# Gate and up of 512 features as one 2x2 block product: seven products in three of eight k-tile pairs, eight PSUM banks, three parts

## The chip, the cores and the metric

The kernel runs on one core of one Trainium2 chip. The metric is the device time of one execution in microseconds (us). Engines are named as in the profile: PE is TensorE, DVE is VectorE, ACT is ScalarE, POOL is GpSimd, SP is the engine that issues most DMAs.

## The reference

Two transformer-like blocks run one after the other on 256 tokens of 2048 features, in float32. The stage that is changed is the feed-forward part of the first block:

```python
h2 = _rmsnorm(x, ffn_norm_w[l])
g, u = jnp.split(jnp.einsum('bsd,df->bsf', h2, w_gate_up[l]), 2, axis=-1)
x = x + jnp.einsum('bsf,fd->bsd', jax.nn.silu(g) * u, w_down[l])
```

`w_gate_up` is 2048 x 11264 (gate in the first 5632 columns, up in the rest), `w_down` is 5632 x 2048. Before this stage stand a gated recurrence, a short convolution and the output projection `w_out`; after it come a second block with attention and a long convolution, and a last norm.

## The kernel before

Every large product is computed with operands split into two float32r parts, high and low: `x = xh + xl`, `w = wh + wl`, and `x w` is taken as `xh wh + xh wl + xl wh`. The split of a weight tile is made on the chip: SP loads 512 KB (two k-tiles of 128 rows by 512 columns) into a `raw` buffer, ACT rounds it into `wh` (L63, by way of `act`), and DVE writes `wl = raw - wh` (L54, by way of `tt`). `split` (L105) does this. It runs at a priority raised by 4000, so that the planner, which orders each engine's list at build time, puts it ahead of the ordinary work. There are four `wh`/`wl` buffer pairs (`wsp`), and four `raw` buffers, eight in the feed-forward stage (`wraw`, `wraw2`, taken in turn).

There are two forms of the product. `proj` (L132) keeps tokens on the output's partitions: the token tile is the stationary operand, the weights move, and each token half takes three 512-column matmuls per k-tile (L149 to L151). `proj_t` (L160) keeps features on the output's partitions: a 128 x 128 block of the weights is stationary, and the high and low parts of all 256 tokens move past it in one matmul of 512 columns (L177), then the low weights meet the high tokens in one of 256 columns (L178; L174 and L175 for the last k-tile). `proj_t` then adds the two halves of its four banks by one ACT copy and one DVE addition each (L182, L183).

The feed-forward stage (L592 to L622) walks 11 groups f of 512 features, in two parts of six and five. For each f it calls `proj_t` for gate, multiplies by the token scale `rs1b` (the reciprocal root of the norm, spread along the free axis by L217), applies Silu, calls `proj_t` for up, multiplies, and splits h into a unit `u` (high and low parts, four k-tiles by 256 tokens). After each part, `proj` multiplies the part's units with `w_down` for four chunks of 512 output columns, and `residual` (L574) adds the result to `X` on DVE. The norm weight is folded into the units `x1u`, which `unit_from` (L87) builds from transposes of `X` (L82) chunk by chunk in the output projection.

PSUM has eight banks: five in `pmm` (matmul results of `proj` and `proj_t`) and three in `phd` (transposes, small products; taken by `bank`). `proj_t` takes four banks at a time, `proj` two.

## Time and profile before

| what | us |
|---|---|
| median of three runs | 1621.42 (1620.3 to 1622.43) |
| the profiled execution | 1621.36 |
| its span (first to last instruction) | 1619.7 |
| PE busy | 1605.1 (99%) |
| DVE busy | 1099.3 (68%) |
| ACT busy | 845.6 (52%) |

The profile lists, for each group of instructions of one line and shape, the count, the busy time, the mean duration and the idle time of the engine just ahead of them with what ended it. The timeline lists instructions by start, neighbours of one group merged into one line with a count. Durations of pipelined instructions overlap, so the spacing of starts tells what one of a stream costs. The windows give the busy time of each engine in a stretch; the column PEclk is the granted clock as a share of 2.4 GHz.

### The profile page before, as it was taken

The page shows a single profiled execution, that of the slowest core. Times are in us where ns is not written, and L with a number is a line of the kernel's source. Part 1 is how long each engine was busy: PE and PEld are TensorE (multiplying, and loading weights), DVE is VectorE, ACT ScalarE, POOL GpSimd, SP SyncE. Part 2 cuts the span into 40 slices and gives each one's busy share as a digit, 9 for nine tenths or more (in the row PEclk, how much of TensorE's full clock was granted, in tenths as well). Part 3 has the DMA queues.
Part 4 walks back from the last instruction along what each step waited for, and adds up shares of the span by engine and source line. Part 5 has one row for each costly group of instructions (what it writes and reads, how often), then busy time and mean ns, then how long its engine had stood idle before and what let it go on. Part 6 is the DMA issues. An engine that isn't in the chain of part 4 may idle for free. (4 is left out here: it accounts for less than half of the span.)

```text
span 1619.7 us, 23619 instructions
## 1 busy us (share of the span) xinstructions
PE 1605.1 (99%) x9152; PEld 1448.8 (89%) x9152; DVE 1099.3 (68%) x1495; ACT 845.6 (52%) x1125; POOL 21.2 (1%) x57
## 2 busy tenths in 40 slices
PE   8999999999999999999999999999999999999998
PEld 7999999999988999999888999998889889998987
DVE  8769768765766666666554566665658999766854
ACT  5657557544544554545444454545446445655743
POOL 2000000000000000000000000000000000000000
PEclk9999999999999999999999999999999999999999
DMA  8765565556696666665666566666547567656564
GB/s 291 219 196 156 152 186 170 152 176 206 208 308 212 193 199 204 198 200 193 216 201 203 183 207 208 207 200 202 197 144 247 157 194 217 188 156 195 165 214 142
DMA packets 166897, 318.45 MB, mean 197 GB/s; under 512 B 12248, under 2 KB 13168, under 8 KB 166784
## 3 DMA queue, kind: packets, MB, share of 16 engines
q1 hardware_dynamic: 164304, 312.19, 61.1%
q10 hardware_dynamic: 2032, 4.60, 0.8%
q8 instruction: 72, 1.18, 0.3%
q14 instruction: 41, 0.34, 0.1%
q0 software_dynamic: 448, 0.14, 0.1%
HBM read 313.74 MB, written 3.15 MB: 196 GB/s over the span
## 5 line engine op out<-in xcount | busy, mean ns | idle before, releaser
L54 DVE TENSOR_TENSOR wl<-raw,wh 128x1024 fp32r<-128x1024 f32 (+1 forms) x580 | 700.8, 1220 | 434.3 <-ACT wh L63 430.4
L63 ACT ACTIVATE wh<-raw 128x1024 fp32r<-128x1024 f32 (+1 forms) x580 | 603.9, 1054 | 603.4 <-PE p L177 268.4
L177 PE MATMUL p<-u,wh 128*128 128x512 f32 x2712 | 891.0, 383 | 0.8 <-DVE sg L54 0.6
L178 PE MATMUL p<-u,wl 128*128 128x256 f32 x2712 | 712.7, 274 | 1.0 <-DVE wl L54 0.9
L177 PEld LDWEIGHTS p<-u,wh 128*128 128x128 f32 x2712 | 507.0, 189 | 61.0 <-DVE sg L54 1.1
L178 PEld LDWEIGHTS p<-u,wl 128*128 128x128 f32 x2712 | 519.3, 191 | 13.8 <-DVE wl L54 1.7
L150 PE MATMUL p<-wl,u 128*128 128x512 f32 x736 | 281.2, 383 | 0.0
L151 PE MATMUL p<-wh,u 128*128 128x512 f32 x736 | 277.7, 380 | 1.9 <-DVE u L51 1.9
L149 PE MATMUL p<-wh,u 128*128 128x512 f32 x736 | 277.7, 382 | 1.1 <-ACT u L63 0.6
L149 PEld LDWEIGHTS p<-wh,u 128*128 128x128 f32 x736 | 139.1, 189 | 21.1 <-ACT u L63 1.6
L151 PEld LDWEIGHTS p<-wh,u 128*128 128x128 f32 x736 | 138.8, 189 | 21.3 <-DVE u L51 2.7
L150 PEld LDWEIGHTS p<-wl,u 128*128 128x128 f32 x736 | 139.3, 189 | 19.4 <-DVE wl L54 0.7
L175 PE MATMUL p<-u,wh 128*128 128x512 f32 x184 | 70.7, 384 | 0.0
L63 ACT ACTIVATE low<-p 128x256 f32<-128x256 f32 x184 | 64.1, 375 | 8.7 <-DVE sg L54 1.5
L51 DVE SCALAR_TENSOR_TENSOR acc<-up,cw,acc 128x256 f32<-128x256 f32 x120 | 51.1, 470 | 0.7 <-ACT acc L63 0.7
L174 PE MATMUL p<-u,wl 128*128 128x256 f32 x184 | 50.7, 275 | 0.0
L174 PEld LDWEIGHTS p<-u,wl 128*128 128x128 f32 x184 | 34.8, 189 | 4.8
L149 PE MATMUL p<-wh,x 128*128 128x512 f32 x96 | 36.4, 379 | 0.0
L150 PE MATMUL p<-wl,x 128*128 128x512 f32 x96 | 36.4, 379 | 0.0
L151 PE MATMUL p<-wh,x 128*128 128x512 f32 x96 | 36.4, 379 | 0.0
L54 DVE TENSOR_TENSOR g<-g,rs1b 128x1024 f32<-128x1024 f32 x22 | 27.0, 1225 | 12.7 <-ACT g L63 12.3
L175 PEld LDWEIGHTS p<-u,wh 128*128 128x128 f32 x184 | 35.3, 192 | 0.1
(272 smaller groups left out, 937.5 us busy)
## 6 DMA issues: line engine op xcount, KB each, us to landing
raw<-in_w_in_dram SPq DMA_DIRECT2D x232, 512.0 KB, 4.1
raw<-in_w_gate_up_dram SPq DMA_DIRECT2D x176, 512.0 KB, 4.6
raw<-in_w_down_dram SPq DMA_DIRECT2D x88, 512.0 KB, 4.6
raw<-in_w_out_dram SPq DMA_DIRECT2D x64, 512.0 KB, 4.8
raw<-in_w_mem_kv_dram SPq DMA_DIRECT2D x14, 512.0 KB, 5.8
xp<-in_x_dram SPq DMA_DIRECT2D x4, 512.0 KB, 7.0
X<-in_x_dram SPq DMA_DIRECT2D x4, 512.0 KB, 5.6
mp<-in_mem_dram SPq DMA_DIRECT2D x3, 512.0 KB, 7.5
```

The source lines that it names most:

```text
L51: nc.vector.scalar_tensor_tensor(out=out, in0=in0, scalar=scalar, in1=in1, op0=op0, op1=op1)
L54: nc.vector.tensor_tensor(out=out, in0=a, in1=b, op=op)
L63: nc.scalar.activation(out=out, in_=in_, func=func, **kw)
L149: nc.tensor.matmul(pt[t], lhsT=u[:, k, 0, sl], rhs=mh, start=st, stop=False)
L150: nc.tensor.matmul(pt[t], lhsT=u[:, k, 0, sl], rhs=ml, start=False, stop=False)
L151: nc.tensor.matmul(pt[t], lhsT=u[:, k, 1, sl], rhs=mh, start=False, stop=sp)
L174: nc.tensor.matmul(pt[f][:, :T], lhsT=wl[:, a, fs], rhs=high, start=False, stop=False)
L175: nc.tensor.matmul(pt[f], lhsT=wh[:, a, fs], rhs=both, start=False, stop=True)
L177: nc.tensor.matmul(pt[f], lhsT=wh[:, a, fs], rhs=both, start=st, stop=False)
L178: nc.tensor.matmul(pt[f][:, :T], lhsT=wl[:, a, fs], rhs=high, start=False, stop=False)
```

## The change

Gate and up of one f are computed together, with tokens on the output's partitions (the form of `proj`). For a pair of k-tiles the product is seen as a 2x2 block product: the blocks of the left side are the two token halves by the two k-tiles, those of the right side the two k-tiles by gate and up. Pairs 0, 1, 3, 5 and 6 are multiplied plainly, eight block products each. Pairs 2, 4 and 7 are multiplied by Strassen's scheme in Winograd's form, seven block products each. The products of all pairs add up in eight banks, P1 to P7 and X4: a plain pair adds straight into P2 and P4 (gate) and P3 and X4 (up).

The sums of token blocks (`F`) are made once, in the output projection, from the transposes that make `x1u`. The differences of weight blocks (`Ta`, `Tb`) are made by DVE for each f after the load, in `raw` buffers, and then split like weights. At the end of an f, nine operations combine the eight banks into g and u. h then has tokens on its partitions, so it is transposed on PE ahead of the last pair of the next f, in the bank of X4, whose partial sum has been copied out before. The token scale is now a scalar per partition, and `rs1b` goes. The split weights get two more buffer pairs (`wsx`), the `fp` pool has one buffer where it had two, and the 11 groups run in three parts of four, four and three.

```diff
-    def split(w, r0, nk, c0, n, pool=wsp):
+    def load(w, r0, nk, c0, n):
+        raw = raw_tile(nk, n)
+        nc.sync.dma_start(
+            out=raw, in_=w[r0:r0 + nk * 128, c0:c0 + n].rearrange("(k p) n -> p k n", p=128)
+        )
+        return raw
+    def parts_of(raw, pool=None):
+        if pool is None:
+            pool = more_w[0] if more_w else wsp
+            if more_w:
+                more_w.append(more_w.pop(0))
+        wh = pool.tile(list(raw.shape), F32R, tag="wh", name="wh")
+        wl = pool.tile(list(raw.shape), F32R, tag="wl", name="wl")
+        act(wh, raw)
+        tt(wl, raw, wh.bitcast(F32), ALU.subtract)
+        return wh, wl
+    def split(w, r0, nk, c0, n, pool=None):
         with tc.high_priority(4000):
...
+            return parts_of(load(w, r0, nk, c0, n), pool)
...
+    def seven_forms(c):
+        def keep(j, ps):
+            p = 2 * c + j
+            if p not in (2, 4, 7):
+                return
+            x_ = fp.tile([128, CW], F32, tag="s1", name="xs").rearrange("p (a t) -> p a t", a=2)
+            for a in range(2):
+                act(x_[:, a], ps[:, a], scale=col("ffn", 2 * p + a))
+            (a11, a21), (a12, a22) = ((x_[:, a, :128], x_[:, a, 128:]) for a in range(2))
+            s_ = fp.tile([128, CW], F32, tag="u2", name="ss").rearrange("p (i t) -> p i t", i=4)
+            tt(s_[:, 0], a21, a22, ALU.add)
+            tt(s_[:, 1], s_[:, 0], a11, ALU.subtract)
+            tt(s_[:, 2], a11, a21, ALU.subtract)
+            tt(s_[:, 3], a12, s_[:, 1], ALU.subtract)
+            F = fp.tile([128, 4, 2, 128], F32R, tag=f"F{p}", name=f"F{p}")
+            act(F[:, :, 0], s_)
+            tt(F[:, :, 1], s_, F[:, :, 0].bitcast(F32), ALU.subtract)
+            sums7[p] = F
...
-        x1u.append(unit_from(xk(c), lambda k, c=c: col("ffn", 4 * c + k)))
+        x1u.append(unit_from(xk(c), lambda k, c=c: col("ffn", 4 * c + k), keep=seven_forms(c)))
...
-    rs1b = along_free(rs1, fp, "rs1b")
     more_raw.extend([wraw, ff.enter_context(tc.tile_pool(name="wraw2", bufs=4))])
+    wsx = ff.enter_context(tc.tile_pool(name="wsx", bufs=2))
+    more_w.extend([wsp, wsp, wsx, wsp, wsp, wsx])
+    def tri(pt, left, right, st, sp):
+        (xh, xl), (wh, wl) = left, right
+        mh, ml = in_turn(wh), in_turn(wl)
+        nc.tensor.matmul(pt, lhsT=xh, rhs=mh, start=st, stop=False)
+        nc.tensor.matmul(pt, lhsT=xh, rhs=ml, start=False, stop=False)
+        nc.tensor.matmul(pt, lhsT=xl, rhs=mh, start=False, stop=sp)
+    def hidden_pre(f, before_last):
+        P1, P2, P6, P7, P5 = [mm_bank() for i in range(5)]
+        P3, P4, X4 = [bank([128, CW]) for i in range(3)]
...
+        for p in order:
...
+            if p not in sums7:
+                for (b0, b1), c0 in (((P2, P4), f * CW), ((P3, X4), DFF + f * CW)):
+                    wh, wl = split(w_gate_up, r0, 2, c0, CW)
+                    for a in range(2):
+                        for t, b in enumerate((b0, b1)):
+                            prod(b, x_(a, t), (wh[:, a], wl[:, a]), b is X4 and p == last_plain and a == 1)
+                continue
+            if end:
+                x4 = fp.tile([128, CW], F32, tag="x4", name="x4")
+                with tc.high_priority(4000):
+                    act(x4, X4)
+                before_last(X4)
+            F = sums7[p]
+            with tc.high_priority(4000):
+                g_ = load(w_gate_up, r0, 2, f * CW, CW)
+                u_ = load(w_gate_up, r0, 2, DFF + f * CW, CW)
+                B1 = parts_of(g_)
+                Ta, Tb = raw_tile(2, CW), raw_tile(2, CW)
+                tt(Ta[:, 0], u_[:, 0], g_[:, 0], ALU.subtract)
+                tt(Ta[:, 1], u_[:, 1], u_[:, 0], ALU.subtract)
+                W13 = parts_of(Ta)
+                tt(Tb[:, 0], u_[:, 1], Ta[:, 0], ALU.subtract)
+                tt(Tb[:, 1], g_[:, 1], Tb[:, 0], ALU.subtract)
+                W24 = parts_of(Tb)
+                B22 = parts_of(u_[:, 1:2])
...
+            prod(P1, x_(0, 0), at(B1, 0), end)
+            prod(P2, x_(1, 0), at(B1, 1), end)
+            prod(P5, form(0), at(W13, 0), end)
+            prod(P7, form(2), at(W13, 1), end)
+            prod(P6, form(1), at(W24, 0), end)
+            prod(P4, x_(1, 1), at(W24, 1), end)
+            prod(P3, form(3), at(B22, 0), end)
...
+        with tc.high_priority(4000):
+            act(s1, P1)
+            tt(g[:, 0], P2, s1, ALU.add)
+            tt(u2, P6, s1, ALU.add)
+            tt(u3, P7, u2, ALU.add)
+            tt(g[:, 1], P4, u3, ALU.add)
+            tt(u2, P5, u2, ALU.add)
+            tt(u3, P5, u3, ALU.add)
+            tt(u2, P3, u2, ALU.add)
+            tt(u3, u3, x4, ALU.add)
+        for t, up_ in enumerate((u2, u3)):
+            act(g[:, t], g[:, t], AF.Silu, scale=rs1[:, t:t + 1])
+            stt(two(h[:, t]), ordered(up_), rs1[:, t:t + 1], ordered(g[:, t]), ALU.mult, ALU.mult)
+        return h
+    def turn(h, u):
+        def run(ps):
+            ps = ps.rearrange("p (a t) -> p a t", a=2)
+            for j in range(2):
+                for a in range(2):
+                    for t in range(NT):
+                        nc.tensor.transpose(
...
+                unit_split(u, ps, 2 * j, 2)
+        return run
...
-    for part in (range(0, 6), range(6, 11)):
+    for part in (range(0, 4), range(4, 8), range(8, 11)):
         gu = []
+        waiting = lambda ps: None
         for f in part:
-            g = fp.tile([128, 4, T], F32, tag="g", name="g")
-            proj_t(dense(x1u), w_gate_up, f * CW, g)
-            tt(g, g, rep(rs1b, 4), ALU.mult)
-            act(g, g, AF.Silu)
-            tt(g, g, rep(rs1b, 4), ALU.mult)
-            h = fp.tile([128, 4, T], F32, tag="hd", name="hd")
-            proj_t(dense(x1u), w_gate_up, DFF + f * CW, h)
-            tt(h, h, g, ALU.mult)
...
+            h = hidden_pre(f, waiting)
+            gu.append((new_unit(), f * CW))
+            waiting = turn(h, gu[-1][0])
+        waiting(bank([128, CW]))
         for c in range(4):
             residual(proj(gu, w_down, c * CW), c)
```

## Rows read from the trace of the kernel before

**Rows 1.** The page's engines, and PE's longest sum of waits (us, times, longest)

```profile
PE 1605.1 (99%) x9152; PEld 1448.8 (89%) x9152; DVE 1099.3 (68%) x1495; ACT 845.6 (52%) x1125; POOL 21.2 (1%) x57
...
PE p L151 <- DVE u L51: 1.9, 2, 1.2
```

**Rows 2.** Window: length, busy us of PE, PEld, DVE, ACT, POOL, then clock

```profile
523.00:1240.00 717.00, 716.86 (x4058) 649.02 (x4057) 445.38 (x480) 348.23 (x425) 2.58 (x6) 1.00 0.62 200
```

**Rows 3.** Timeline (start, duration) of PE: first and eighth 512-column matmul of eight

```profile
699.80 0.38 PE L177 MATMUL p<-u,wh 128*128 128x512 f32 x1
...
702.09 0.38 PE L177 MATMUL p<-u,wh 128*128 128x512 f32 x1
```

**Rows 4.** The tile hd: durations (min, median, max), first and last start

```profile
L54 DVE TENSOR_TENSOR hd<-hd,g x11: 1225/1225/1226, 569.4 to 1112.9; 128x1024 f32<-128x1024 f32 x11
```

**Rows 5.** Timeline of PE in a down pass: first and sixteenth of sixteen matmuls

```profile
799.74 0.38 PE L149 MATMUL p<-wh,x 128*128 128x512 f32 x1
...
802.98 0.38 PE L149 MATMUL p<-wh,x 128*128 128x512 f32 x1
```

**Rows 6.** Timeline of PE round eight transposes in the output projection

```profile
462.46 0.38 PE L82 MATMUL h<-ident,X 128*128 128x128 f32 x2
462.60 0.46 PE L151 MATMUL p<-wh,u 128*128 128x512 f32 x1
462.90 0.82 PE L82 MATMUL h<-ident,X 128*128 128x128 f32 x6
463.47 0.46 PE L149 MATMUL p<-wh,u 128*128 128x512 f32 x1
463.77 0.38 PE L150 MATMUL p<-wl,u 128*128 128x512 f32 x1
```

**Rows 7.** Timeline of PE round the products of rs1b

```profile
531.02 0.38 PE L177 MATMUL p<-u,wh 128*128 128x512 f32 x1
531.24 0.61 PE L217 MATMUL h<-ident,rs 128*128 128x128 f32 x4
...
531.79 0.38 PE L177 MATMUL p<-u,wh 128*128 128x512 f32 x1
```

**Rows 8.** Groups of DVE and ACT by shape: busy us, mean ns, idle before

```profile
L54 DVE TENSOR_TENSOR wl<-raw,wh 128x1024 fp32r<-128x1024 f32 x576 | 698.3, 1224 | 434.3 <-ACT wh L63 430.4 <-PE p L178 2.9
L54 DVE TENSOR_TENSOR X<-p,X 128x512 f32<-128x512 f32 x31 | 19.9, 681 | 1.6 <-PE p L927 1.6
L51 DVE SCALAR_TENSOR_TENSOR X<-X,rsf,rw 128x512 f32<-128x512 f32 x8 | 5.5, 745 | 0.0
...
L63 ACT ACTIVATE wh<-raw 128x1024 fp32r<-128x1024 f32 x576 | 601.5, 1057 | 600.8 <-PE p L177 268.4 <-PE p L151 199.6 <-PE p L175 35.3
```

**Rows 9.** Timeline of DVE: back to back, a dependent step, a wait

```profile
868.86 1.28 DVE L54 TENSOR_TENSOR X<-p,X 128x512 f32<-128x512 f32 x2
...
1091.18 0.75 DVE L54 TENSOR_TENSOR g<-p,low 128x256 f32<-128x256 f32 x2
1091.96 1.23 DVE L54 TENSOR_TENSOR g<-g,rs1b 128x1024 f32<-128x1024 f32 x1
1094.31 1.23 DVE L54 TENSOR_TENSOR g<-g,rs1b 128x1024 f32<-128x1024 f32 x1 [1.12 <-ACT g L63]
1096.47 3.50 DVE L54 TENSOR_TENSOR wl<-raw,wh 128x1024 fp32r<-128x1024 f32 x3 [0.94 <-ACT wh L63]
```

**Rows 10.** Windows, columns as in group 2, of three other stretches

```profile
470.00:500.00 30.00, 30.00 (x144) 26.30 (x144) 17.43 (x19) 13.96 (x16) 0.17 (x1) 1.00 0.72 229
545.00:587.00 42.00, 42.00 (x259) 38.61 (x258) 26.89 (x30) 22.32 (x27) 0.00 (x0) 1.00 0.63 199
1320.00:1360.00 40.00, 40.00 (x217) 35.51 (x216) 40.00 (x72) 21.27 (x28) 0.00 (x0) 1.00 0.70 214
```

**Rows 11.** The page's DMA issues: KB each, median us to landing

```profile
raw<-in_w_gate_up_dram SPq DMA_DIRECT2D x176, 512.0 KB, 4.6
```

**Rows 12.** Groups of DVE by shape between 1320 and 1360 us

```profile
L51 DVE SCALAR_TENSOR_TENSOR acc<-up,cw,acc 128x256 f32<-128x256 f32 x43 | 18.4, 466 | 0.0
```

More of the change, by code (lines that the diff above doesn't have):

```diff
@@ L85, in transposed, with unit_from @@
         return ps
-    def unit_from(src, scale, u=None, js=range(2)):
+    def unit_from(src, scale, u=None, js=range(2), keep=None):
         u = u or new_unit()
@@ L90, in unit_from @@
             ps = transposed(src, j)
+            if keep is not None:
+                keep(j, ps)
             for a in range(2):
@@ L103, in tile_two_blocks, with raw_tile @@
     more_raw = []
-    def split(w, r0, nk, c0, n, pool=wsp):
-        with tc.high_priority(4000):
-            raw = (more_raw[-1] if more_raw else wraw).tile([128, nk, n], F32, tag="raw", name="raw")
-            more_raw.reverse()
-            nc.sync.dma_start(
-                out=raw, in_=w[r0:r0 + nk * 128, c0:c0 + n].rearrange("(k p) n -> p k n", p=128)
-            )
-            wh = pool.tile([128, nk, n], F32R, tag="wh", name="wh")
-            wl = pool.tile([128, nk, n], F32R, tag="wl", name="wl")
-            act(wh, raw)
-            tt(wl, raw, wh.bitcast(F32), ALU.subtract)
-        return wh, wl
+    more_w = []
+    def raw_tile(nk, n):
+        raw = (more_raw[-1] if more_raw else wraw).tile([128, nk, n], F32, tag="raw", name="raw")
+        more_raw.reverse()
+        return raw
[4 more added lines that the diff above has]
+        )
+        return raw
+    def parts_of(raw, pool=None):
[9 more added lines that the diff above has]
+    def split(w, r0, nk, c0, n, pool=None):
+        with tc.high_priority(4000):
+            return parts_of(load(w, r0, nk, c0, n), pool)
     def mm_bank():
@@ L582, in tile_two_blocks @@
     x1u = []
+    ff = ExitStack()
+    fp = ff.enter_context(tc.tile_pool(name="fp", bufs=1))
+    sums7 = {}
+    def seven_forms(c):
[16 more added lines that the diff above has]
+            sums7[p] = F
+        return keep
     for c in range(4):
@@ new lines, in tile_two_blocks, with prod, x_, at @@
+    more_w.extend([wsp, wsp, wsx, wsp, wsp, wsx])
[8 more added lines that the diff above has]
+        P3, P4, X4 = [bank([128, CW]) for i in range(3)]
+        begun = set()
+        order = [0, 1, 2, 3, 4, 5, 6, 7]
+        last_plain = max(p for p in order if p not in sums7)
+        def prod(pt, left, right, end=False):
+            tri(pt, left, right, id(pt) not in begun, end)
+            begun.add(id(pt))
+        for p in order:
+            u, a0 = x1u[p // 2], 2 * (p % 2)
+            r0, end = 256 * p, p == order[-1]
+            def x_(a, t):
+                sl = slice(t * 128, (t + 1) * 128)
+                return u[:, a0 + a, 0, sl], u[:, a0 + a, 1, sl]
+            if p not in sums7:
[23 more added lines that the diff above has]
+                B22 = parts_of(u_[:, 1:2])
+            def at(w, a):
+                return w[0][:, a], w[1][:, a]
+            def form(i):
+                return F[:, i, 0], F[:, i, 1]
+            prod(P1, x_(0, 0), at(B1, 0), end)
[5 more added lines that the diff above has]
+            prod(P3, form(3), at(B22, 0), end)
+        s1 = fp.tile([128, CW], F32, tag="s1", name="s1")
+        u2 = fp.tile([128, CW], F32, tag="u2", name="u2")
+        u3 = fp.tile([128, CW], F32, tag="u3", name="u3")
+        g = fp.tile([128, NT, CW], F32, tag="g", name="g")
+        h = fp.tile([128, NT, CW], F32, tag="hd", name="hd", bufs=2)
+        with tc.high_priority(4000):
[12 more added lines that the diff above has]
+        return h
@@ new lines, in turn @@
+    def turn(h, u):
[5 more added lines that the diff above has]
+                        nc.tensor.transpose(
+                            out=ps[:, a, t * 128:(t + 1) * 128],
+                            in_=h[:, t, (2 * j + a) * 128:(2 * j + a + 1) * 128], identity=ident,
+                        )
+                unit_split(u, ps, 2 * j, 2)
+        return run
@@ L621, in tile_two_blocks @@
     more_raw.clear()
+    more_w.clear()
     ff.close()
```

9 lines of the change are left out of this document (removed).

## The prediction

> **What bounds the kernel now.** I read the page's list of engines first: TensorE (PE) is busy 99% of the span, VectorE (DVE) 68%, ScalarE (ACT) 52% [rows 1]. Busy records of a pipelined engine overlap, so the next view is the list of what PE waited for: its longest sum is 1.9 us in the whole span [rows 1]. Nothing that feeds PE is late, so the time is the sum of PE's starts. The windows say the same of the stage that the change touches: from 523 to 1240 us PE is full, DVE has 445 of 717 us and ACT 348, and the granted clock is 1.00, the 2.4 GHz level [rows 2]. So each start that PE loses there is time gained, as long as DVE and ACT still deliver the split weights on time. The prediction weighs these two sides.
>
> **PE, before.** One call of `proj_t` runs 64 pairs of a 512-column and a 256-column matmul; gate and up of one f (512 features) are two calls, 128 pairs. Seven pairs take 702.09 - 699.80 = 2.29 us [rows 3], 0.327 each, so one f costs 128 x 0.327 = 41.9 us. Cross-check: the product `hd<-hd,g` of the first f starts at 569.4, that of the eleventh at 1112.9 [rows 4]; between them lie ten f and one down pass of six units, 6 x 4 x 24 = 576 matmuls at 3.24/15 = 0.216 us [rows 5], 124.4 us; (543.5 - 124.4)/10 = 41.9. The two agree.
>
> **PE, after.** Every product is now the three 512-column matmuls of `tri`, the form of the down pass, 0.216 each [rows 5]. Five plain pairs have 2 matrices x 2 k-tiles x 2 token halves x 3 = 24 matmuls, three seven-product pairs 7 x 3 = 21: 183 x 0.216 = 39.5 us. New are the transposes of h, 2 x 4 blocks. Eight transposes with two matmuls between them run from 462.46 to 463.77 [rows 6]: 1.31 - 2 x 0.216 = 0.88 us, also per f. Sum 40.4; the saving is 1.5 us per f, 11 x 1.51 = 16.6 us. (Without the nine products that Strassen saves, nothing would remain: 192 x 0.216 + 0.88 = 42.4.) The four L217 products of `rs1b` go as well: with them 0.77 us pass from 531.02 to 531.79, a plain pair takes 0.33 [rows 7], so 0.44. The down matmuls keep their number in three passes. The sum goes against the profiled execution, 1621.36 us (span 1619.7 and 1.7 around it), 0.06 us from the median 1621.42. With PE alone: 1621.4 - 16.6 - 0.4 = 1604.3 us.
>
> **DVE, the price.** Durations are 1.224 us for a split of 1024, 0.681 for an addition of 512, 0.745 for a product of 512 with a row scalar [rows 8]. Back to back an operation starts before the one ahead has ended: three splits take 3.50 us, so (3.50 - 1.22)/2 = 1.14 each, two PSUM additions 1.28, so the first counts 0.60 [rows 9]; I take 0.60 for every addition and split of 512 (those in SBUF too) and 0.66 for the scaled product. Per f:
> - plain pairs: 5 x 2 splits x 1.14 = 11.4;
> - seven-product pairs: each has 3 splits of 1024, 1 of 512 and 4 additions for Ta and Tb, 3 x (3.42 + 0.60 + 2.40) = 19.3;
> - evacuation: 8 additions 4.8, the two products into h 1.3, two splits of the transposed h 1.2.
>
> That is 38.0. An operation that reads what the one just ahead of it wrote starts 0.03 us after that one's end (1091.18 + 0.75, then 1091.96 [rows 9]), 0.12 later than back to back; at most seven such a f, 0.8. So 38.8 us of DVE stand against 40.4 of PE: 96%, where one f of before has 26.9 in 42 [rows 10]. ACT rises to 19 splits of 1024 at 1.06, 3 of 512 and six smaller passes, some 26 of 40 us [rows 8], with room.
>
> Can DVE run so full while PE is fed? One stretch says yes: from 1320 to 1360 us DVE is busy 40.0 of 40 us and PE 40.0 [rows 10]. But much of DVE's work there is not awaited at once (18.4 us are `acc` steps of the convolution [rows 12]); after the change nearly all of it is. What DVE can lose are hand-overs: ACT must write wh before DVE writes wl. Where DVE has nothing else queued it idles 1.12 us (`g<-g` behind the Silu [rows 9]). Each Ta and Tb is made by DVE, rounded by ACT and taken up by DVE again: six such per f, and one more at the evacuation, which needs ACT's s1. With k of these seven left unfilled, PE waits 38.8 + 1.12k - 40.4 = 1.12k - 1.6 us per f: none for k up to 1, 0.64 for two, 1.76 for three, 2.9 for four. I take two: the one at the evacuation, which stands in front of the next f's splits on DVE's queue, and one in pair 2, which follows it while the lead is shortest. Pairs 4 and 7 come after plain pairs, where DVE needs 2 x 1.14 us of PE's 5.2. There are six wh/wl pairs of buffers for the 22 weight tiles of one f, and a seven-product pair takes four, so the lead is never over six tiles. Cost 11 x 0.64 = 7.0 us; bounds 0 and 31.7 (four).
>
> **Banks.** All eight PSUM banks hold one f. The next f starts in P2 and P4. P2 is free once DVE has added it (its product ends five products, 3.2 us, ahead of the last one); P4 needs the chain P6, P7, P4, three dependent additions of 0.7 behind P6, which ended 1.3 us before the end: about 0.8 us after it, while P2 takes 0.65 (both token halves 1.3). P3 and P4 then have up to 5 us of cover in P2 and X4 if the list is ordered so. Nothing in the trace of before has all banks in use; I bound it by 0 and by one split of 1.14 us queued ahead of the additions in each of the 8 successions within a part, 9 us, and take 0: the transposes at 462 us stand between matmuls of the next product [rows 6], so the order is already built round such waits.
>
> **What lies beside other work.** Sums F for pairs 2, 4 and 7 are made in the output projection: some 1.9 us of DVE and 1.6 of ACT each (four additions, a split of 512, three ACT passes), where DVE has 17.4 and ACT 14.0 of 30 us [rows 10]: no cost. The third down pass adds 8 additions of 0.68 on DVE; the stage has DVE at 445 of 717 us [rows 2]: no cost. At a part's end the last h goes through evacuation, Silu, transposes and splits, some 11 us, while the other units give PE 3 x 5.2 us (2 x 5.2 in the last part): 0 to 1 us. At the stage's start P4 and X4 wait for banks of the transposes of the last x1u chunk: 0 to 2. I take 1 us for all edges. Loads are the same 16 per f, but Ta and Tb pass through the same eight raw buffers, so SP's queue issues later; a load lands 4.6 us after issue [rows 11], eight buffers are some 14 us of work, and behind a waiting load only further loads of this stage are queued: no cost, else it adds to k.
>
> **Forecast.** 1604.3 + 7.0 + 1 = 1612 us.
>
> **Rivals.**
> - PE alone sets the pace (k of 1 or less): 1604 to 1606. For it: the stretch with DVE at 40 of 40 [rows 10]. Against: much of DVE's work there has no due time so close.
> - Three hand-overs open: 1604.3 + 19.4 = 1624, no change.
> - DVE becomes the bound and the change is slower: four or more open, two in pair 2 and one each in pair 4 and at the evacuation: 1604.3 + 31.7 = 1636. It turns slower than before by 0.2% (3.2 us) from (1624.7 - 1604.3)/11 = 1.85 us of waiting per f, 3.1 hand-overs. For it: six buffers, of which four go to one pair. Against: ACT has 14 us per f free, so it can round early.
> - Each DVE operation takes its whole duration: 10 x 1.224 + 9 x 1.224 + 12 x 0.68 + 3 x 0.68 + 8 x 0.68 + 2 x 0.745 + 2 x 0.68 = 41.7 us per f, more than PE's 40.4: 1621.4 - 0.4 - 11 x 0.2 = 1619, no change. The rows speak against it: three splits take 3.50 us, not 3.67 [rows 9]. The Trainium skill (VectorE: DVE Perf Modes, section The DRAIN you can't avoid) says that after each operation the next does not start until the pipe has emptied (it points to an earlier start where the next is not held), and its rules advise few operations; read strictly it makes this rival the forecast, and the rows do not.
> - The saved products are not saved, since PE stands at the transposes: their second batch needs the bank of the first, read by ACT and DVE, 1.3 us; with nothing put between, 11 x 1.5 = 16.5 us: 1621. Against: [rows 6].
>
> **Chances.** Forecast 0.40, PE alone 0.22, three hand-overs 0.09, slower 0.17, whole durations 0.05, transposes 0.07. A measurement of this kernel tells about 0.2% from no change. Faster by more is 0.62, within 0.2% is 0.09 + 0.05 + 0.07 = 0.21, slower 0.17. The range runs from 1603, PE alone, to 1628, where about half of the slower case is left out; the two banks' and edges' upper bounds lie inside.
>
> **What would show it.** In the profile after: the spacing of `tri` matmuls 0.216; 8 transposes per f; the period from one h to the next 41.0 (40.4 if PE alone, 42.2 or more if three hand-overs are open); DVE over 90% busy in this stage; PE's waits, if any, named after wl, some 7 us in sum. If PE waits for P2 or P4 to be read, the bank step is wrong; if the spacing differs, the PE sum is; if DVE's sum per f is over 40, its additions cost more than I took.

## The result, and the profile after

The changed kernel takes 1634.3 us (median of four runs, 1633.3 to 1635.8) against 1621.5 us before: a ratio of 1.008, 95% interval [1.0068, 1.0093]. It is slower; 1612 was forecast, in a range that ended at 1628. TensorE alone would give 1604.3 by the prediction's sum, so there are 30 us to explain, of which the forecast held 8. (The profiled execution took 1633.3 us, with a span of 1631.5.)

The page of the kernel after, its engines and the head of its chain of waits, answers to [rows 1]:

```profile
PE 1596.9 (98%) x8433; PEld 1410.5 (86%) x8433; DVE 1238.2 (76%) x1715; ACT 885.5 (54%) x1156; POOL 23.6 (1%) x57
...
PE 77%; DVE 14%; DMA 4%; issue 3%; ACT 1%; DVEq 0%; ACTq 0%; POOLq 0%; POOL 0%
```

The chain that ended last leaves TensorE: 14% of it is VectorE and 4% DMA, nearly all of that loads of gate and up weights. Next, the waits of the kernel after: engine, line, releaser, then us in sum, times, longest.

```profile
PE p L646 <- DVE wl L54: 11.5, 16, 2.1
PE p L645 <- DVE g L54: 3.2, 2, 1.6
...
PE p L645 <- ACT wh L63: 1.7, 1, 1.7
PE p L645 <- DVE u L54: 1.4, 4, 0.4
...
DVE raw L54 <- DMA raw<-in_w_gate_up_dram: 55.7, 25, 4.7
```

TensorE's four waits in this stage sum to 17.8 us. The longest wait by far isn't TensorE's: VectorE stands 55.7 us for loads to land, always ahead of the additions that make Ta (`raw<-raw`); before, DVE's weight splits waited for ScalarE (430 of 434 us) and for no load [rows 8]. The loads themselves aren't slower; the page's row on them, against 4.6 us before [rows 11]:

```profile
raw<-in_w_gate_up_dram SPq DMA_DIRECT2D x176, 512.0 KB, 4.5
```

The windows, with columns as in [rows 2]: the whole stage, which takes longer than before, and one period within it, from the first addition of one evacuation (`g<-p,s`) to that of the next:

```profile
523.00:1252.00 729.00, 710.85 (x3343) 612.18 (x3341) 578.98 (x687) 384.72 (x449) 3.49 (x6) 1.00 0.63 198
...
609.15:653.58 44.43, 41.65 (x192) 34.97 (x191) 38.62 (x47) 24.30 (x28) 0.00 (x0) 1.00 0.62 196
```

VectorE's work is 38.62 us in this period, where the ledger said 38.8 per f. The period is 44.4 instead of 41.0, and VectorE idles 5.81 us of it. It is one of the two longest: the eight periods inside a part run from 40.6 to 45.0 us, 42.3 in the mean, so the loss does not fall on every f alike. The timeline of DVE in the second half of this period says where (start, duration, what, and in brackets the idle time before it); then the load on SP's queue that ended the longer wait, and TensorE some us later:

```profile
635.44 1.29 DVE L54 TENSOR_TENSOR raw<-raw 128x512 f32<-128x512 f32 x2 [1.16 <-DMA raw<-in_w_gate_up_dram]
...
640.13 3.48 DVE L54 TENSOR_TENSOR wl<-raw,wh 128x1024 fp32r<-128x1024 f32 x3
648.17 1.29 DVE L54 TENSOR_TENSOR raw<-raw 128x512 f32<-128x512 f32 x2 [4.56 <-DMA raw<-in_w_gate_up_dram]
...
643.64 0.37 SPq L115 DMA_DIRECT2D raw<-in_w_gate_up_dram  x1
...
655.45 0.48 PE L646 MATMUL p<-wl,u 128*128 128x512 f32 x1 [1.58 <-DVE wl L54]
```

These lines show how the loss comes about in this period. The third of three splits ends at 640.13 + 3.48 = 643.61. SP issues the next load at 643.64, because that split was the last reader of the raw buffer which the load takes. It lands at 648.2; The next operation in VectorE's list needs it, so VectorE idles 4.56 us. The two waits, 1.16 + 4.56 = 5.72, are all of the 5.81 us. TensorE doesn't stand at that moment, for it has split weights in hand; it stands from some six us after the load has landed, at the change from one f to the next, for a `wl`. The other changes of f agree in part. In all five at which TensorE stands more than 2.3 us in sum, VectorE had waited 3.2 to 4.7 us for a load within the 9 us ahead of the evacuation. But at the end of the first f of each part it had waited 4.3 to 4.4 us as well, and TensorE stands less than 0.4 there.

### The profile page after: what moved, and what is told of

Read it like the earlier page. It is cut to its first block, busy times and chain, and to the rows that moved or that the text cites. A ratio compares the mean times of both kernels' runs of the same rounds, so it can differ in the third digit from the quotient of the medians.

```text
span 1631.5 us, 22403 instructions
## 1 busy us (share of the span) xinstructions
PE 1596.9 (98%) x8433; PEld 1410.5 (86%) x8433; DVE 1238.2 (76%) x1715; ACT 885.5 (54%) x1156; POOL 23.6 (1%) x57
## 4 chain that ended last, share of the span: by engine, by line
PE 77%; DVE 14%; DMA 4%; issue 3%; ACT 1%; DVEq 0%; ACTq 0%; POOLq 0%; POOL 0%
PE p L194 18%; PE p L167 10%; PE p L168 10%; PE p L166 10%; PE p L195 9%; DVE wl L54 8%; DMA raw<-in_w_gate_up_dram 4%; PE h L646 3%; PE h L647 3%; PE h L645 3%; DVE raw L54 2%; PE h L446 2%; PE p L646 2%; PE p L647 1%; PE p L645 1%
## 5 line engine op out<-in xcount | busy, mean ns | idle before, releaser
L194 PE MATMUL p<-u,wh 128*128 128x512 f32 x1392 | 458.7, 383 | 0.6 <-DVE sg L54 0.6
L195 PE MATMUL p<-u,wl 128*128 128x256 f32 x1392 | 365.6, 274 | 1.0 <-DVE wl L54 0.9
L167 PE MATMUL p<-wl,u 128*128 128x512 f32 x832 | 317.0, 382 | 0.9 <-DVE wl L54 0.9
L168 PE MATMUL p<-wh,u 128*128 128x512 f32 x832 | 312.6, 381 | 2.0 <-DVE u L51 2.0
L166 PE MATMUL p<-wh,u 128*128 128x512 f32 x832 | 311.8, 381 | 1.1 <-ACT u L63 0.6
L194 PEld LDWEIGHTS p<-u,wh 128*128 128x128 f32 x1392 | 260.1, 190 | 31.3 <-DVE sg L54 1.1
L195 PEld LDWEIGHTS p<-u,wl 128*128 128x128 f32 x1392 | 266.5, 191 | 8.4 <-DVE wl L54 1.7
L646 PE MATMUL h<-wl,u 128*128 128x512 f32 x363 | 138.0, 380 | 0.1
L647 PE MATMUL h<-wh,u 128*128 128x512 f32 x363 | 137.1, 379 | 0.0
L645 PE MATMUL h<-wh,u 128*128 128x512 f32 x363 | 135.3, 381 | 0.0
L54 DVE TENSOR_TENSOR raw<-raw 128x512 f32<-128x512 f32 x132 | 87.2, 685 | 56.6 <-DMA raw<-in_w_gate_up_dram 55.7
L646 PE MATMUL p<-wl,u 128*128 128x512 f32 x176 | 69.1, 392 | 10.8 <-DVE wl L54 10.7
L645 PEld LDWEIGHTS h<-wh,u 128*128 128x128 f32 x363 | 68.6, 189 | 10.1 <-DVE u L54 0.7
L647 PEld LDWEIGHTS h<-wh,u 128*128 128x128 f32 x363 | 68.6, 189 | 9.6
L645 PE MATMUL p<-wh,u 128*128 128x512 f32 x176 | 65.8, 385 | 3.2 <-DVE g L54 3.2
L647 PE MATMUL p<-wh,u 128*128 128x512 f32 x176 | 67.3, 382 | 0.0
```

Of the source, the lines that this page charges most:

```text
L54: nc.vector.tensor_tensor(out=out, in0=a, in1=b, op=op)
L166: nc.tensor.matmul(pt[t], lhsT=u[:, k, 0, sl], rhs=mh, start=st, stop=False)
L167: nc.tensor.matmul(pt[t], lhsT=u[:, k, 0, sl], rhs=ml, start=False, stop=False)
L168: nc.tensor.matmul(pt[t], lhsT=u[:, k, 1, sl], rhs=mh, start=False, stop=sp)
L194: nc.tensor.matmul(pt[f], lhsT=wh[:, a, fs], rhs=both, start=st, stop=False)
L195: nc.tensor.matmul(pt[f][:, :T], lhsT=wl[:, a, fs], rhs=high, start=False, stop=False)
```

## Experiments

"TensorE's sum" is the sum of matmul starts by the prediction's prices: 1604.3 us with three seven-product pairs. Ratios are against the kernel before, whose medians beside these runs are 1621.3 to 1622.0 us.

**1. Is TensorE's sum right? No seven-product pair.**

```diff
-            if p not in (2, 4, 7):
+            if True:
...
-            act(s1, P1)
...
+        for t, (gp, up_) in enumerate(((P2, P3), (P4, X4))):
+            act(g[:, t], gp, AF.Silu, scale=rs1[:, t:t + 1])
```

> The changed kernel with no seven-product pair at all: all eight pairs plain in the token-major form, four banks that ScalarE and VectorE read directly, the bank of P1 for the transposes, three parts. It leaves Strassen's scheme out and keeps the rest. TensorE: 192 x 0.216 + 0.88 = 42.35 us per f, 0.5 more than before, 1626 in all; VectorE has about 24 us per f. By the prediction's TensorE sum, 1625 to 1628 without stalls. If the token-major form itself with its transposes and readout brings the stalls, over 1635.

Measured: 1626.4 us (1625.8 to 1627.3), ratio 1.0026 [1.0016, 1.0036], as the outcome without stalls. The window of 42 us in its stage:

```profile
604.00:646.00 42.00, 42.00 (x201) 36.78 (x200) 21.76 (x21) 18.88 (x20) 0.00 (x0) 1.00 0.68 200
```

TensorE is full, and the time is the sum: 42.4 us per f by the prediction against 41.9 before, 11 x 0.5 - 0.4 = 5 us slower than 1621.4. So the token-major form, the transposes and the third down pass cost what was said.

**2. The third down pass alone.** The kernel before, in three parts:

```diff
-    for part in (range(0, 6), range(6, 11)):
+    for part in (range(0, 4), range(4, 8), range(8, 11)):
```

> The kernel before with the stage in three parts of four, four and three groups instead of two of six and five. The prediction held the third down pass to cost nothing (VectorE's eight more additions lie beside TensorE's work): 1621 to 1623. If the third part is where some of the changed kernel's loss comes from, over 1625.

Measured: 1621.3 us, ratio 0.9996 [0.9987, 1.0006], as expected. It is free.

**3. Is it the amount of VectorE's work? Two seven-product pairs instead of three.**

```diff
-            if p not in (2, 4, 7):
+            if p not in (3, 7):
```

> The changed kernel with two seven-product pairs (3 and 7) in place of three (2, 4 and 7). TensorE alone: 186 x 0.216 + 0.88 = 41.06 us per f, 1611.5 us in all. VectorE's work per f falls from 38.7 to about 34.8 us and 20 raw buffers are filled per f instead of 22. Theory A: some landings are still waited for, 1612 to 1622. Theory B: VectorE has 6 us of slack, 1612 to 1616. Theory C (banks, which are held and read out in the same way): the stalls of about 28 us stay less little, 1630 to 1640.

Measured: 1635.6 us, ratio 1.0084 [1.0069, 1.0099]. One period of it, and from the timeline the row of DVE just ahead of it:

```profile
607.07:652.27 45.20, 41.33 (x182) 34.97 (x181) 34.95 (x42) 22.54 (x26) 0.00 (x0) 0.92 0.58 187
```

```profile
604.72 1.29 DVE L54 TENSOR_TENSOR raw<-raw 128x512 f32<-128x512 f32 x2 [3.88 <-DMA raw<-in_w_gate_up_dram]
...
629.99 1.23 DVE L54 TENSOR_TENSOR wl<-raw,wh 128x1024 fp32r<-128x1024 f32 x1 [2.37 <-ACT wh L63]
```

VectorE has 3.7 us less to do per f, and this period is no shorter: 10 us of it are idle. Of these 1.4 go to loads; 8.7 are waits for ScalarE's roundings in the middle of the period, like the second row, while TensorE stands only near the period's start (2.02 and 1.84 us). Against TensorE's own sum for two pairs, 1611.5, 24 us are lost, where the change loses 30. The theory that VectorE simply has too much to do falls. But the theory of loads had said 1612 to 1622 and missed; the time lies in the range named for the banks, which this run alone can't rule out.

**4. Six and ten raw buffers instead of eight.** Room for the two more comes from `hd` with one buffer instead of two and from the small tile `vm`.

With ten (six has `bufs=2` and the list `wraw2, wraw, wraw`):

```diff
-    vm = const.tile([16, 128], F32, name="vm")
+    vm = lowp.tile([16, 128], F32, tag="low", name="vm")
...
-    more_raw.extend([wraw, ff.enter_context(tc.tile_pool(name="wraw2", bufs=4))])
+    wraw2 = ff.enter_context(tc.tile_pool(name="wraw2", bufs=6))
+    more_raw.extend([wraw2, wraw, wraw2, wraw, wraw2])
...
-        h = fp.tile([128, NT, CW], F32, tag="hd", name="hd", bufs=2)
+        h = fp.tile([128, NT, CW], F32, tag="hd", name="hd")
```

> The changed kernel with six raw buffers in the stage. Theory A (loads): VectorE's wait for landings at least doubles (over 110 us in sum) and the time rises by more than 15 us, to over 1650. Theory B (VectorE's work, hand-overs): little change, below 1640. Theory C (banks): none, 1632 to 1636.

> The changed kernel with ten raw buffers in the feed-forward stage in place of eight (one h buffer instead of two makes the room). Theory A, the loads: between 609 and 653 us of the changed kernel VectorE is busy 38.7 of 44.5 us and idle 5.7 us at the head of Ta additions that wait for a load to land, and the load waits for a raw buffer that VectorE has only just given back. With ten buffers a load is issued some 3.5 us earlier, so most of the 55.7 us that VectorE waits for landings in sum goes (below 20) and the time falls to 1608 to 1618. Theory B, VectorE's own work and its hand-overs to ScalarE: the idle time moves to another wait, 1628 to 1636. Theory C, the eight PSUM banks: no change, 1632 to 1636.

Measured: six 1645.0 us, 1.0143 [1.0128, 1.0159]; ten 1618.6 us, 0.9982 [0.9973, 0.9991]. The same stretch of the period with six, then with ten:

```profile
606.83:654.50 47.67, 44.86 (x196) 37.53 (x195) 40.21 (x50) 26.07 (x30) 0.00 (x0) 0.93 0.59 191
```

```profile
601.64:644.27 42.63, 41.22 (x194) 35.32 (x193) 38.80 (x47) 24.12 (x29) 0.00 (x0) 1.00 0.66 200
```

With no engine's work changed, two buffers fewer cost 11 us and two more give 16. With ten VectorE idles 42.63 - 38.80 = 3.8 us of a period, 2 less than with eight. The direction is that of the theory of loads, and both times just miss its ranges (over 1650, and 1608 to 1618). But what it said of VectorE's waits is not borne out. Its waits for landings, with six and with ten:

```profile
DVE raw L54 <- DMA raw<-in_w_gate_up_dram: 46.3, 17, 5.3
```

```profile
DVE raw L54 <- DMA raw<-in_w_gate_up_dram: 38.4, 31, 3.9
```

They were to rise over 110 us with six and fall below 20 with ten. The slowest of the three kernels has fewer of them than the one with eight (55.7), so the time does not follow their sum.

**5. One more pair of wh and wl tiles** (seven instead of six; `hd` and `vm` as in experiment 4).

```diff
-    wsx = ff.enter_context(tc.tile_pool(name="wsx", bufs=2))
-    more_w.extend([wsp, wsp, wsx, wsp, wsp, wsx])
+    wsx = ff.enter_context(tc.tile_pool(name="wsx", bufs=3))
+    more_w.extend([wsp, wsx, wsp, wsx, wsp, wsx, wsp])
```

> The changed kernel with seven wh/wl buffer pairs in the stage in place of six, the raw buffers left at eight (one h buffer makes the room). Theory A (loads wait for raw buffers): little change, 1629 to 1635. Theory D (the lead of six weight tiles is too short for the burst of evacuation and seven-product pair): a good part of the 28 us of stalls goes, 1612 to 1624.

Measured: 1627.5 us, ratio 1.0034 [1.0021, 1.0047]: 7 us better than the change and between the two outcomes named. A longer lead covers part of the idle time; it doesn't remove it. This kernel gave up the same tiles as the one with ten buffers, and the two steps together gave 7 us, so these tiles are unlikely to be what made ten buffers 16 us faster; they were not tried alone.

**6. Ta and Tb made by GpSimd,** with eight and with ten raw buffers.

```diff
-                tt(Ta[:, 0], u_[:, 0], g_[:, 0], ALU.subtract)
+                nc.gpsimd.tensor_tensor(out=Ta[:, 0], in0=u_[:, 0], in1=g_[:, 0], op=ALU.subtract)
...
```

> The changed kernel with the four additions for Ta and Tb on GpSimd in place of VectorE. The wait for a landing then holds GpSimd's list and not VectorE's, and VectorE has 7.2 us per f less to do (31.6 of TensorE's 40.4). Theory A, in the form that a late load blocks VectorE's list and with it the splits that come behind: 1608 to 1618. If the late load itself is what TensorE waits for (its own tile comes late, whoever adds): 1624 to 1634. If GpSimd's additions are slow or slow VectorE down: over 1636.

> Both: additions for Ta and Tb on GpSimd and ten raw buffers (one h buffer). With ten buffers alone the time was 1618.5. If what is left there is VectorE's work and list, 1606 to 1612; if what is left is the burst at the succession of two f, whoever does it, 1615 to 1620; if GpSimd is slow, above 1620.

Measured: 1629.0 us, 1.004 [1.0024, 1.0055], and 1623.0 us, 1.0007 [0.9997, 1.0016]. The first lies in the range named for a load that comes late whoever adds, the second in that for a slow GpSimd. With ten buffers it is worse than leaving the additions on VectorE. Groups of GpSimd and of DVE in this stage (busy us, mean ns, idle before) say why; the first three are of the kernel with eight buffers:

```profile
L687 POOL TENSOR_TENSOR raw<-raw 128x512 f32<-128x512 f32 x32 | 55.4, 1733 | 372.3 <-DMA raw<-in_w_gate_up_dram 347.9 <-DVE X L54 7.4 <-DVE g L54 6.3
...
L54 DVE TENSOR_TENSOR wl<-raw,wh 128x1024 fp32r<-128x1024 f32 x306 | 427.1, 1412 | 135.1 <-ACT wh L63 132.1 <-DMA raw<-in_w_down_dram 1.2
L54 DVE TENSOR_TENSOR u<-p,u 128x512 f32<-128x512 f32 x33 | 22.4, 677 | 0.0
```

and these two of the changed kernel:

```profile
L54 DVE TENSOR_TENSOR wl<-raw,wh 128x1024 fp32r<-128x1024 f32 x306 | 367.4, 1218 | 85.4 <-ACT wh L63 82.1 <-DMA raw<-in_w_down_dram 2.4
...
L54 DVE TENSOR_TENSOR u<-p,u 128x512 f32<-128x512 f32 x33 | 22.4, 679 | 0.0
```

The waits for landing go to GpSimd, and yet only 5 us are gained. An addition takes 1.7 to 2.0 us there (means of the four lines), and VectorE's splits, whose operands both lie in SBUF, grow from 1218 to 1412 ns in the mean (306 x 0.194 = 59 us), so that VectorE's busy sum on the page is no smaller (1239.7 us, in the changed kernel 1238.2).

**7. Are the banks the rest? Splits held back behind the evacuation.** The four splits of the first seven-product pair wait for u3 of the f before (one element of each wh is first written from it), so that the additions that free the banks come sooner.

```diff
+        if gate is not None:
+            nc.gpsimd.tensor_copy(out=wh[0:1, 0, 0:1], in_=gate[0:1, 0:1])
         act(wh, raw)
```

> Eight raw buffers as in the changed kernel; the splits of the first seven-product pair of an f may not start before the last but one addition of the f before (one element of each of its four wh tiles is first written from u3 by GpSimd). Theory A (the loads that wait for their raw buffer set the time, the interleaved evacuation costs the rest): the splits are only moved, raw buffers come free no earlier, so at most the 1.7 us per succession that remained with ten buffers can go, eight times, and the delayed splits can take it back: 1620 to 1634 us. Theory C (the evacuation of the eight banks, one split of 1.14 us between any two additions, is the whole cost): the 28 us go nearly all, 1606 to 1612 us. If the gate itself delays the weights: above 1634 us.

> Ten raw buffers and the gate. With ten raw buffers alone (1618.6 us) a succession kept 1.7 to 2 us, in which the banks P4, P3 and X4 waited to be read while VectorE alternated additions with splits. Theory: if that alternation is the rest of the cost, 8 successions x 1.7 us = 13.6 us go: 1605 us. If what remains is again a late weight, the gate moves it from the banks to the first product of the pair: 1616 to 1622 us.

Measured: 1644.5 us, 1.0141 [1.0125, 1.0156], and with ten buffers 1632.2 us, 1.0064 [1.0049, 1.0079]. Both are 10 to 14 us slower than without the gate: as the last outcome named for eight buffers, and as none of those for ten. There the waits have moved; TensorE's row at a change of f:

```profile
610.18 1.12 PE L743 MATMUL h<-ident,hd 128*128 128x128 f32 x4 [3.00 <-DVE u L54]
```

Now the second batch of transposes stands 3 us for VectorE to read the first, which it does only after a split and three additions of its list; a load held them up by no more than 0.12 us. The gate moved several things at once and tells nothing of the banks.

**8. Twelve raw buffers** (two in a borrowed unit, and four parts to have one to spare), without and with the gate.

```diff
+    spare = new_unit().bitcast(F32).rearrange("p k a t -> p (k a t)")
...
-    for part in (range(0, 4), range(4, 8), range(8, 11)):
+    for part in (range(0, 3), range(3, 6), range(6, 9), range(9, 11)):
```

> Twelve raw buffers (two in a spare unit) and four parts (3, 3, 3, 2 of f) instead of three, which costs one more down pass; no gate. Theory A: VectorE's 38 us of waits for landing with ten buffers shrink again; PE waits less after each succession, but the 1.7 us of the banks stay: 1610 to 1617 us. If landing no longer matters at ten: 1617 to 1620 us. A fourth part turns one succession into a part's end (7 successions instead of 8).

> Twelve raw buffers, four parts and the gate: both steps that were put at nothing are repaired. If loads and banks together are the whole loss: the sum for TensorE alone, 1604.3 us, plus 2.4 us of the stage's start: 1604 to 1609 us. If a third thing remains (the ACT hand-overs, the amount of VectorE's work), no better than the run without the gate: 1612 to 1620 us.

Measured: 1640.8 us, 1.0123 [1.0107, 1.014], and 1651.6 us, 1.0188 [1.0173, 1.0204], both above every outcome that had been named. More buffers did not help here. VectorE still stands for loads, in the old pattern (three splits, then a wait for landing); the timeline of DVE without the gate:

```profile
747.61 3.17 DVE L54 TENSOR_TENSOR wl<-raw,wh 128x1024 fp32r<-128x1024 f32 x3
754.77 1.29 DVE L54 TENSOR_TENSOR raw<-raw 128x512 f32<-128x512 f32 x2 [4.00 <-DMA raw<-in_w_gate_up_dram]
```

So the number of buffers alone does not decide. The gate costs time a third time, 11 us. Whether the borrowed tile or the other parts undid the gain was not separated.

**9. The disputed cost by itself: no loads.** All gate and up blocks are split from two tiles loaded once, so the products are not those of the reference; every engine keeps its work (VectorE is busy 1240.4 us, in the changed kernel 1238.2). `hd` and `vm` are as in experiment 4.

```diff
+    fixed = [fixp.tile([128, 2, CW], F32, tag=f"x{i}", name="fixed") for i in range(2)]
...
-                    wh, wl = split(w_gate_up, r0, 2, c0, CW)
+                    with tc.high_priority(4000):
+                        wh, wl = parts_of(fixed[c0 >= DFF])
...
-                g_ = load(w_gate_up, r0, 2, f * CW, CW)
-                u_ = load(w_gate_up, r0, 2, DFF + f * CW, CW)
+                g_, u_ = fixed
```

> Leaves out: every load of gate and up weights but one; all blocks are split from the first 256 rows and 512 + 512 columns, which stay in two tiles of their own, so no split and no addition waits for a load or a raw buffer to be read; the work of the engines is unchanged. If waiting for loads is the loss, all 28 us go: 1605 to 1608 us. If loads are the 16 us that ten buffers gave and no more: 1617 to 1620 us. If the amount or order of VectorE's work is the loss: 1628 us or more.

Measured: 1608.7 us (1607.8 to 1609.3), ratio 0.9917 [0.9902, 0.9932]. The stage, and one period:

```profile
523.00:1252.00 729.00, 728.99 (x3507) 637.99 (x3506) 590.27 (x692) 397.28 (x465) 2.58 (x6) 1.00 0.27 84
...
603.73:644.78 41.05, 41.05 (x194) 35.31 (x193) 36.06 (x44) 24.07 (x29) 0.00 (x0) 1.00 0.08 27
```

TensorE is full from 523 to 1252 us, with 590 us of VectorE's work beside it. VectorE idles here too, 5 us of this period, but for another reason; a row of its timeline, and ScalarE's wait behind it:

```profile
643.64 1.22 DVE L54 TENSOR_TENSOR wl<-fixed,wh 128x1024 fp32r<-128x1024 f32 x1 [2.81 <-ACT wh L63]
```

```profile
ACT wh L63 <- PE h L655: 127.9, 95, 4.3
```

ScalarE waits for a wh tile that TensorE still reads: both are as far ahead as the six pairs allow. 1634.3 - 1608.7 = 25.7 us of the loss go when loads and the raw buffers that they wait for go. The measured time is 0.7 us above the outcome named for this, and far below the others. The gain is not one lucky order of the list: a second kernel without loads (experiment 10) takes 1607.7. What the tiles `hd` and `vm` have in it was not tried; against experiment 5, with the same two tiles, eight buffers and a longer lead, 18.8 us go. The last evacuation of the stage begins 25 us earlier than in the changed kernel: 16 of these lie in the eight changes of f inside a part, 5.3 at the ends of two parts, and 3.7 ahead of the first evacuation. What is left, 4.4 us above TensorE's sum, stands outside the periods of f, which take 40.3 us in the mean here, against 40.4 in the sum; I call it edges.

**10. Banks read by ScalarE,** in the changed kernel, with ten raw buffers, and without loads.

```diff
             act(s1, P1)
             tt(g[:, 0], P2, s1, ALU.add)
+            act(g[:, 1], P4)
+            act(h[:, 0], P3)
...
-            tt(g[:, 1], P4, u3, ALU.add)
+            tt(g[:, 1], g[:, 1], u3, ALU.add)
...
-            tt(u2, P3, u2, ALU.add)
+            tt(u2, h[:, 0], u2, ALU.add)
```

> Eight raw buffers. ScalarE copies P4 into g[:, 1] and P3 into the h tile as soon as they end, and the additions read these copies: the two banks that the next f needs first no longer wait for VectorE's chain, at no change of the weights' order or memory; two more ScalarE copies of about 0.6 us per f. Theory (loads cost some 16 us, late banks the other 13): 1634 - 13 = 1621 us. If banks only hide behind the late weights: 1630 to 1634 us. If banks are the whole loss: 1606 us.

> The same copies with ten raw buffers. With ten buffers alone a succession kept 1.7 to 2 us of stalls. If those are the banks P4 and P3: 1618.6 - 13 = 1605 us, below both kernels. If they are late weights that show up in the banks only by accident: 1616 to 1619 us.

> Leaves out the same loads, and has the two copies of banks by ScalarE. If loads and banks are all that the sum missed: 1604 to 1607 us (TensorE alone 1604.3). What stays above that is a third cost, such as late products of weights by VectorE's order.

Measured: 1629.7 us, 1.005 [1.0035, 1.0065]; 1615.9 us, 0.9963 [0.995, 0.9976]; 1607.7 us, 0.9909 [0.9893, 0.9926]. The copies give 4.6, 2.7 and 1.0 us, the last within the spread of the runs. Where loads come in time the banks cost about nothing; where they don't, the copies gain a few us, which is little beside what a new order of the list alone may move. The 13 us that I had put on the banks after experiment 4 were not theirs.

**11. Three raw buffers per seven-product pair instead of four:** Tb is written over g.

```diff
-                Ta, Tb = raw_tile(2, CW), raw_tile(2, CW)
+                Ta, Tb = raw_tile(2, CW), g_
```

> The changed kernel with Tb written over g and nothing else: eight raw buffers, 19 taken per f, 8 x 40.4/19 = 17.0 us round, between the 14.7 us of the changed kernel (30 us above TensorE's own sum) and the 18.4 us of ten buffers (14 us above it). Theory of the round trip: 1620 to 1628 us. If the number of buffers taken does not count: 1634 us as the changed kernel.

> Ten raw buffers, the two bank copies by ScalarE, and Tb written over g (whose values are no longer needed), so a seven-product pair takes three raw buffers instead of four: 19 per f instead of 22. Theory (a raw buffer comes round too soon for its load: buffers times the time per buffer is 8 x 42/16 = 21.0 us before, 8 x 40.4/22 = 14.7 us in the changed kernel and 18.4 us with ten): here 10 x 40.4/19 = 21.3 us, as before, so nearly all of the remaining 11.5 us go: 1605 to 1609 us. If Tb, which now waits for the splits of g, brings a wait of its own, or if it is not the number of buffers that counts: 1614 to 1620 us.

Measured: with eight buffers and nothing else changed 1617.0 us, 0.997 [0.9958, 0.9982], 17 us better than the change by one line, and better than the 1620 to 1628 of the theory of the round trip. With ten buffers and the bank copies 1627.5 us, 1.0038 [1.0025, 1.005], 12 us worse than without it and in neither range named. A period with eight buffers; then waits of TensorE and ScalarE in the second kernel; then ScalarE's in the first:

```profile
604.15:646.97 42.82, 40.91 (x190) 34.61 (x189) 38.80 (x48) 24.37 (x29) 0.00 (x0) 1.00 0.61 193
```

```profile
PE p L647 <- ACT wh L63: 6.9, 11, 1.1
...
ACT wh L63 <- DVE raw L54: 71.8, 17, 7.7
```

```profile
ACT wh L63 <- DVE raw L54: 86.9, 30, 6.2
```

With Tb over g ScalarE stands for VectorE's Ta and Tb, 72 us in sum with ten buffers (3.9 us with ten buffers and the copies alone). TensorE then waits for a rounding 11 times, 6.9 us. But the faster kernel with eight buffers has the same wait of ScalarE, 87 us, so this wait alone does not tell why ten buffers are slower here. That stays open.

Three of these versions are faster than both kernels, by 0.2 to 0.4% of the time before: ten buffers (1618.6 us), the same with the bank copies (1615.9 us), and Tb over g alone (1617.0 us).

## Why the prediction was wrong, point by point

- **TensorE's sum: right.** The kernel without seven-product pairs came within half a us of it (experiment 1), the one without loads within 4.4 (experiment 9). (The saving of 1.51 us per f is 1.45 to 1.50 by the prediction's own figures, under 1 us in all.) The transposes are 88, and their second batch did not stand; the rival "saved products are not saved" is out for this kernel.
- **VectorE's ledger: right in sum,** 38.62 us in a period against 38.8. One term was too small: the product into h, of two operands read in permuted order, takes 921 ns instead of 745 (below), 2 x 0.18 = 0.35 us per f. The splits of three in 3.48 us, (3.48 - 1.22)/2 = 1.13 each, again speak against the rival of whole durations. By the Trainium skill (VectorE: DVE Perf Modes, section The DRAIN you can't avoid), read strictly, an estimated 3 x 1.22 = 3.66 us would pass there; the trace does not agree with that reading.
- **Loads: the step that failed.** "No cost, else it adds to k" was one sentence of the paragraph on what lies beside other work. The term was put at nothing, and 25.7 of the 30 us stand behind it (experiment 9). The numbers were in the prediction: a load lands 4.6 us after issue [rows 11], and VectorE's slack was 40.4 - 38.8 = 1.6 us per f. What was missing is their comparison. A load is issued when VectorE releases a buffer, so if the planned list has no other work for VectorE at that point, one such load idles it for 4.6 us (4.56 in the timeline above), three times the slack of an f. I spent the slack on hand-overs of 1.12 us and never set it against this larger piece. I also counted loads ("the same 16 per f") and not takings of a buffer: Ta and Tb raise these from 16 to 22 per f, so a buffer comes round after 8 x 40.4/22 = 14.7 us, where before it was 8 x 42/16 = 21.0. "Some 14 us of work" stood in the text, without the 21 beside it. That loads cost the time is shown; the way there, by VectorE's idling, is read from the trace of one kernel. The sum of these waits does not give the time: it is 46.3 us in the kernel of 1645.0 (six buffers), 55.7 in the changed kernel, 32.1 in that of 1635.6 (two pairs), 38.4 in that of 1618.6 (ten buffers) and 24.4 in that of 1617.0 (Tb over g).
- **Hand-overs (k): 7.0 us forecast, about none found.** Without loads the six hand-overs Ta, wh, wl and the one at the evacuation are all still there, and TensorE does not stand in the stage. The rival "VectorE becomes the bound" named 1636 us, which is near by luck: its mechanism, four open hand-overs, is not what happened. Its point of decision, 1.85 us of TensorE's waiting per f, was passed: 30/11 = 2.7.
- **Banks: taken as 0, and about 0** where nothing else is late (1.0 us, experiment 10), 3 to 5 us beside late loads. The sign named against this step did come: TensorE waits 3.2 us for P2 to be read (`PE p <- DVE g`, twice) and 1.4 for other banks. Both waits for P2 stand behind a load, as VectorE reads P2 late after it. Its timeline ahead of the first, whose end is TensorE's row at 864.52 below:

```profile
858.88 1.29 DVE L54 TENSOR_TENSOR raw<-raw 128x512 f32<-128x512 f32 x2 [4.00 <-DMA raw<-in_w_gate_up_dram]
...
863.69 0.68 DVE L54 TENSOR_TENSOR g<-p,s 128x512 f32<-128x512 f32 x1
```

- **Edges: 1 us forecast.** Without loads 4.4 us are left above the sum, and that is all that edges and the changes of f have when no load is late. The third down pass is free (experiment 2).
- **What would show it:** the spacing and the ledger came as written; VectorE is at 79% of the stage instead of over 90% because it waits, and TensorE's waits after `wl`, 11.5 us, are the visible end of what its 55.7 us of waits started.

**What stays open.** Ten buffers and Tb over g gave 16 and 17 us, each alone (experiments 4 and 11); twelve buffers, and ten together with Tb over g, did not. Each build gets a newly planned order of the list, and which load meets which wait changes with it; that this is what moves these kernels by 10 us and more is my reading, and no run separates it. That loads and their buffers cost 26 us is shown; a rule that gives the cost from the number of buffers, or from VectorE's waits in sum, is not. Nor is it shown why a late load costs nothing at the end of a part's first f.

## What to carry to other kernels

When a change fills the engine that feeds the bound engine to 96%, set its slack per period (here 1.6 us) against the longest single wait that it can meet, a load behind a late release (here 4.6 us), and not only against the short hand-overs. Count how often a buffer is taken per period, intermediates included, and not how many loads there are. And an experiment that removes the suspected resource altogether, as the one without loads, settles in one run how much it costs, where changes of buffers and order each bring a new order of the list with them.

## What the runs showed of the hardware

The group of the products into h in the changed kernel's stage, against 745 ns for a product with a row scalar in [rows 8]:

```profile
L51 DVE SCALAR_TENSOR_TENSOR hd<-u,rs,g 128x512 f32<-128x512 f32 x22 | 20.3, 921 | 0.0
```

Additions on GpSimd lengthened VectorE's splits by 0.19 us in the mean while its additions with a PSUM operand kept theirs (677 and 679 ns, experiment 6). In the trace with eight buffers it is the overlap that counts: splits beside no GpSimd addition take 1.22 us in the mean, those that one overlaps 1.76, and the additions from PSUM 0.68 either way. The Trainium skill (SBUF — State Buffer, section SBUF: two separate sides) says that VectorE's instructions with two SBUF inputs and GpSimd's that read SBUF take one pair of ports in turn, each for the whole instruction. These numbers agree.

TensorE's clock fell after one of its stalls in the changed kernel's stage. The timeline of PE there, and the windows of the period and of the fall (the last three columns are the granted clock, the DMA share and GB/s):

```profile
864.52 0.45 PE L645 MATMUL p<-wh,u 128*128 128x512 f32 x1 [1.59 <-DVE g L54]
865.57 0.60 PE L646 MATMUL p<-wl,u 128*128 128x512 f32 x1 [0.59 <-DVE wl L54]
865.95 0.63 PE L647 MATMUL p<-wh,u 128*128 128x512 f32 x1
866.38 0.63 PE L645 MATMUL p<-wh,u 128*128 128x512 f32 x1
...
868.51 0.71 PE L646 MATMUL p<-wl,u 128*128 128x512 f32 x1
```

```profile
864.00:909.00 45.00, 43.22 (x191) 36.02 (x191) 38.74 (x47) 23.35 (x27) 0.00 (x0) 0.96 0.61 188
...
865.80:869.20 3.40, 3.40 (x9) 2.44 (x9) 3.40 (x5) 0.76 (x2) 0.00 (x0) 0.50 0.83 252
```

After two waits, 1.59 and 0.59 us, matmuls start 0.43 us apart instead of 0.216 at a granted clock of 0.50: the 1.2 GHz level in place of 2.4. From 865.57 to 868.51 seven matmuls take 2.94 us instead of 1.51, so this stall cost 1.4 us more than its waits show. After the waits of 1.73, 1.58 and 2.09 us at three other changes of f in this stage the clock stayed at 1.00.
